# A fused layer's opening: transposed inputs, V's products chunk by chunk over all tokens, and the first norm's factor applied behind them

## The chip, the core and the metric

The kernel runs on one core of one Trainium2 chip. The metric is the device time of one execution in microseconds (us). A core has five engines that run side by side and wait for each other through semaphores: PE (TensorE, matrix products), ACT (ScalarE), DVE (VectorE), POOL (GpSimd) and SP (SyncE, which here only issues DMAs). Each engine takes its instructions strictly in their order, so an instruction that waits holds up everything behind it on its engine. Products land in eight PSUM banks, from which ACT and DVE read them.

## The reference

One layer over 512 tokens of width 1024, in float32. What matters for this change is its opening and one product near the middle:

```python
u = rms_norm(h, g_mix[i])          # x * rsqrt(mean(x*x) + eps) * g
z = u @ w_in[i]                    # q, k, v of two attentions, forget logits, gates
q_a, k_a, v_a, q_b, k_b, v_b, f_b, gate_logits = jnp.split(z, SPLIT_POINTS, axis=-1)
y_a = sliding_window_attention(...) @ w_br_swa[i]
y_b = forgetting_attention(..., f_b + b_forget[i]) @ w_br_fox[i]
...
h = h + ple_gate * (p[i] @ w_ple_proj[i])
```

The norm's factor, one number per token, multiplies every element of that token's row of `u`, and so it can also be multiplied onto a row of a product `(x * g) @ W` after the product. The kernel computes products to float32 accuracy: each operand is split into a high part (rounded to PE's fast float32 format) and the low rest, and each product is the sum of three, high by high, high by low, low by high. A split costs one ACT instruction (the high part) and one DVE instruction (the low part, which waits for the high one).

## The kernel before

Tokens are worked on in four blocks of 128 (`tb`), the width of 1024 in eight chunks of 128 (`k`). The opening, in a scratch pool `s0`, is the part that the change rewrites. For each block `tb`:

- `square1` forms the sum of squares of a row, `rms_rstd` (L359, L362, on POOL) raises it to the power -1/2, one number per token, and `scale1` (L454, DVE) multiplies block, factor and gain.
- `to_uT_pe` (L378) transposes the block on PE in eight 128x128 pieces, and `to_uT_split` (L70 on ACT, L71 on DVE) splits the transposed block out of PSUM into `uh` and `ul`.
- `v_mm` (L474) makes the block's V products for both attentions together with the forget logits: 648 columns, as 320 and 328 in two PSUM banks, eight chunks of three products each, so 48 products per block and 192 in all.
- `v_out` splits the products into `V2` and writes the logits `fl`.

V's weights are split once (`split_v`, L460 and L461). Before the first real product PE runs 20 transposes of an identity matrix (L501) and nine that bring the gain `g_mix` into the shapes wanted.

Behind the opening, `fill` multiplies `uh` and `ul` with the chunks of `w_in` one 128-column unit after the other (L74 to L76, PSUM tag `mm`, two banks): first `ka`, the keys of the sliding attention, 24 products that go through all eight `k`; then `qa`, and so on, mixed with the attention's steps. `unit(key)` hands out a unit's split weights (L324 on ACT, L325 on DVE, four pieces for early units) and splits two units ahead.

The order on PE and POOL is the order of the program text. Within the opening the order on ACT, DVE and SP is also that of the text; behind it a scheduler places instructions on these three and may move some of them between those of the opening. Tiles of later stages take over the memory of `s0` and wait until all that read it there is done.

Near the middle, `p_transposed` transposes `p` on PE (eight pieces, tile `p_tr`) and splits it for the product with `w_ple_proj`.

Of the kernel before, what the change touches and what calls it, by code (L numbers as in the profile page):

```python
# [8 lines left out]
F32 = mybir.dt.float32  # L9
# [5 lines left out]
P = 128  # L15
S = 512
# [10 lines left out]
N_WARM = (14, 3, 3)  # L27

# [22 lines left out]
def layer_kernel(ctx: ExitStack, tc: tile.TileContext, x, p, g_mix, w_in, b_forget, swa_sinks,  # L51
# [5 lines left out]
    p = p[0, 0]  # L57
# [354 lines left out]
    g_bc = s0.tile([P, D], F32, name="g_mix_bc")  # L412
    g_row = s0.tile([KT, P], F32, name="g_row")
    g_col = s0.tile([P, KT], F32, name="g_col")
    wv_h = s0.tile([P, KT, 648], F32R, name="wv_h")
    wv_l = s0.tile([P, KT, 648], F32R, name="wv_l")
    xts, wvs, xn1 = [], [], {}

    def load_x(tb):
        xt = s0.tile([P, D], F32, tag="xt", bufs=3, name=f"x_{tb}")  # L420
        for half in range(2):
            sl = slice(half * 512, half * 512 + 512)
            queue = nc.scalar if tb == 0 and half == 1 else nc.sync
            queue.dma_start(xt[:, sl], x[tb * P:(tb + 1) * P, sl])
            if tb == 0 and half == 0:
                nc.sync.dma_start(g_row, g_mix[0].rearrange("(k q) -> k q", q=P))
        xts.append(xt)

    def load_wv(k):
        src = w_in[k * P:(k + 2) * P, :].rearrange("(k q) c -> q k c", q=P)  # L430
        wv = s0.tile([P, 2, 648], F32, tag="wv_r", bufs=4, name=f"wv_{k}")
        nc.sync.dma_start(wv[:, :, 0:520], src[:, :, C_VB:C_VB + 520])
        nc.sync.dma_start(wv[:, :, 520:648], src[:, :, C_VA:C_VA + 128])
        wvs.append(wv)

    def square1(tb):
        acc = sm.tile([P, 2], F32, tag="acc1", name=f"acc1_{tb}")
        xn = xn1[tb] = s0.tile([P, D], F32, tag="xn", bufs=2, name=f"n1_{tb}_xn")
        nc.scalar.activation(xn[:, 0:512], xts[tb][:, 0:512], AF.Square, scale=1.0 / 32,
                             accum_out=acc[:, 0:1])  # L440
        if tb < 2:
            nc.vector.tensor_tensor_reduce(out=xn[:, 512:], in0=xts[tb][:, 512:],
                                           in1=xts[tb][:, 512:], scale=1.0 / D, scalar=0.0,
                                           op0=ALU.mult, op1=ALU.add, accum_out=acc[:, 1:2])
        else:
            nc.scalar.activation(xn[:, 512:], xts[tb][:, 512:], AF.Square, scale=1.0 / 32,
                                 accum_out=acc[:, 1:2])
        return acc

    def scale1(tb, acc):  # L450
        rs = rms_rstd(acc, f"n1_{tb}")
        for half in range(2):
            sl = slice(half * 512, half * 512 + 512)
            nc.vector.scalar_tensor_tensor(xn1[tb][:, sl], xts[tb][:, sl], rs,  # L454
                                           gps[half] if tb < 2 else g_bc[:, sl],
                                           ALU.mult, ALU.mult)

    def split_v(k):
        src = wvs[k // 2][:, k % 2]
        nc.scalar.copy(wv_h[:, k], src)  # L460
        nc.vector.tensor_tensor(wv_l[:, k], src, wv_h[:, k].bitcast(F32), ALU.subtract)  # L461
# [3 lines left out]
    def v_mm(tb, k, nk=1):  # L465

        ts_ = slice(tb * P, (tb + 1) * P)
        if k == 0:
            vps[tb] = (psA.tile([P, 320], F32, tag="mm", bufs=2, name=f"va_{tb}"),
                       psA.tile([P, 328], F32, tag="sc", bufs=3, name=f"vb_{tb}"))  # L470
        for n, (u, w) in enumerate(((uh, wv_h), (uh, wv_l), (ul, wv_h))):
            for kk_ in range(k, k + nk):
                for ps, c0, c1 in ((vps[tb][0], 0, 320), (vps[tb][1], 320, 648)):
                    nc.tensor.matmul(ps, u[:, kk_, ts_], w[:, kk_, c0:c1],  # L474
                                     start=kk_ == 0 and n == 0, stop=kk_ == KT - 1 and n == 2)

    def v_out(tb):
        pa, pb = vps[tb]
        for src, h0, n in ((pa, 0, 5), (pb[:, 0:192], 5, 3), (pb[:, 200:328], 8, 2)):
            v3 = src.rearrange("q (h d) -> q h d", d=HD)  # L480
            hi_lo(V2[tb][:, h0:h0 + n, 0:HD], V2[tb][:, h0:h0 + n, HD:2 * HD], v3)
        nc.vector.tensor_tensor(fl[:, tb, :], pb[:, 192:200], bf_bc, ALU.add)

    with tc.manual_schedule(engines={ET.Activation, ET.DVE, ET.SP}):
        load_x(0)
        load_wv(0)
        load_wv(2)
        load_x(1)
        load_wv(4)
        load_wv(6)  # L490
        load_x(2)
        load_x(3)
        bcast_row(bf_bc, b_forget[0])
        bcast_row(sink_bc, swa_sinks[0])


        warm = psA.tile([P, 4, P], F32, tag="tr", bufs=3, name="warm")

        def warm_up(n):
            for j in range(n):  # L500
                nc.tensor.transpose(warm[:, j % 4, :], ident, ident)  # L501
# [39 lines left out]
        for tb in range(1, NT):  # L541
# [8 lines left out]
            if tb == 2:  # L550
                unit("ka")
# [966 lines left out]
```

## Time and profile before

| | us |
|---|---|
| median of 3 runs | 715.99 (715.10 to 716.78) |
| the profiled execution | 717.25 |
| its span on the core | 715.3 |
| PE busy | 704.4 (98% of the span) |
| DVE, ACT, POOL busy | 532.7, 450.2, 84.8 |
| first V product on PE starts | 8.98 |
| first `ka` product on PE starts | 41.90 |
| first `qa` product on PE starts | 47.37 |

Times within the profile count from the span's start. A row of the timeline gives the start, the duration, the engine, the line of the program, the operation, what it writes and reads with sizes, and, where the engine stood idle before it, how long and what ended that. Where a row groups several instructions (x4), its duration reaches from the first's start to the last's end; neighbours on ACT and DVE overlap by some hundredths of a us. The chain of waits follows the end of the program back, at each step to what released the waiting instruction.

### The profile page before, as it was taken

The page shows a single profiled execution, that of the slowest core. Times are in us where ns is not written, and L with a number is a line of the kernel's source. Part 1 is how long each engine was busy: PE and PEld are TensorE (multiplying, and loading weights), DVE is VectorE, ACT ScalarE, POOL GpSimd, SP SyncE. Part 2 cuts the span into 40 slices and gives each one's busy share as a digit, 9 for nine tenths or more (in the row PEclk, how much of TensorE's full clock was granted, in tenths as well). Part 3 has the DMA queues.
Part 4 walks back from the last instruction along what each step waited for, and adds up shares of the span by engine and source line. Part 5 has one row for each costly group of instructions (what it writes and reads, how often), then busy time and mean ns, then how long its engine had stood idle before and what let it go on. Part 6 is the DMA issues. An engine that isn't in the chain of part 4 may idle for free.

```text
span 715.3 us, 11466 instructions
## 1 busy us (share of the span) xinstructions
PE 704.4 (98%) x4229; PEld 626.4 (88%) x4229; DVE 532.7 (74%) x908; ACT 450.2 (63%) x839; POOL 84.8 (12%) x124
## 2 busy tenths in 40 slices
PE   8999999999999999999999999999999999999995
PEld 7988888888888998888899889988999789988885
DVE  6557888877696556545789985899579966997565
ACT  6547888779863554344788736874477546875452
POOL 1011211100001200001510102010300021010101
PEclk9999999999999999999999999999999999999998
DMA  9256456670364795450885598739894699079002
GB/s 288 70 164 159 115 125 158 151 196 1 119 206 118 147 320 181 152 172 31 238 188 193 111 288 160 239 86 256 185 253 119 152 243 233 34 148 351 3 22 96
DMA packets 74055, 115.67 MB, mean 162 GB/s; under 512 B 6664, under 2 KB 44560, under 8 KB 74000
## 3 DMA queue, kind: packets, MB, share of 16 engines
q1 hardware_dynamic: 65936, 86.24, 38.0%
q0 software_dynamic: 7776, 28.32, 21.5%
q8 instruction: 33, 0.54, 0.3%
q10 hardware_dynamic: 288, 0.39, 0.2%
q14 instruction: 22, 0.18, 0.1%
HBM read 72.93 MB, written 4.19 MB: 108 GB/s over the span
## 4 chain that ended last, share of the span: by engine, by line
PE 86%; DVE 6%; DMA 4%; issue 2%; ACT 1%; POOL 0%; SPq 0%; POOLq 0%; DVEq 0%; ACTq 0%
PE pf L74 5%; PE pf L76 5%; PE pf L75 5%; PE s_6x L1331 3%; PE s_0x L1331 3%; PE h_sc L760 3%; PE s_2x L1331 2%; PE h_pv L830 2%; PE h_tr L818 2%; PE psm L76 2%; PE psm L74 2%; PE psy L74 2%; PE psy L75 2%; PE psm L75 2%; PE psy L76 2%
## 5 line engine op out<-in xcount | busy, mean ns | idle before, releaser
L298 POOL DMA_DIRECT2D wq<-wq x24 | 21.8, 936 | 166.8 <-DVE u70l L325 25.9
L778 ACT ACTIVATE s<-s,h_nm 128x128 f32<-128x128 f32 (+1 forms) x64 | 32.6, 512 | 5.9 <-DVE h_nm L771 5.1
L71 DVE TENSOR_TENSOR h_ptl<-h_tr,h_pth 128x512 fp32r<-128x512 f32 (+2 forms) x40 | 22.9, 604 | 4.0 <-ACT h_pth L70 3.6
L359 POOL TENSOR_SCALAR n_ms<-acc 128x1 f32<-128x1 f32 x15 | 5.6, 373 | 163.8 <-ACT junk L1083 105.4
L70 ACT CAST h_pth<-h_tr 128x512 fp32r<-128x512 f32 (+2 forms) x40 | 19.4, 523 | 1.8 <-PE h_tr L818 1.4
L70 ACT CAST u<-n_tr 128x512 fp32r<-128x512 f32 (+2 forms) x26 | 12.6, 519 | 11.8 <-PE n_tr L1139 5.6
L474 PE MATMUL va<-wv_h,u 128*128 128x320 f32 x64 | 20.0, 317 | 0.0
L818 PE MATMUL h_tr<-ident,s 128*128 128x128 f32 x136 | 19.6, 277 | 0.2
L474 PE MATMUL vb<-wv_h,u 128*128 128x328 f32 x64 | 19.6, 313 | 0.0
L71 DVE TENSOR_TENSOR u<-n_tr,u 128x512 fp32r<-128x512 f32 (+2 forms) x26 | 15.0, 603 | 5.8 <-ACT u L70 5.7
L298 POOL DMA_DIRECT2D wgw<-wgw x8 | 7.1, 971 | 102.3 <-DVE u25l L325 77.7
L1083 ACT ACTIVATE junk<-h_sb 128x512 f32<-128x512 f32 x16 | 10.1, 630 | 12.6 <-DVE h_sb L1073 10.1
L830 PE MATMUL h_pv<-h_pth,v 128*128 128x256 f32 (+1 forms) x64 | 17.3, 291 | 0.0
L830 PE MATMUL h_pv<-h_ptl,v 128*128 128x256 f32 (+1 forms) x64 | 16.9, 305 | 0.3 <-DVE h_ptl L71 0.3
L818 PEld LDWEIGHTS h_tr<-ident,s 128*128 128x128 f32 x136 | 15.1, 141 | 2.0 <-ACT s L798 0.5
L1420 DVE TENSOR_TENSOR sgp<-sgp,pp 128x512 f32<-128x512 f32 (+1 forms) x9 | 5.7, 632 | 14.2 <-ACT sgp L1419 14.2
L1073 DVE TENSOR_TENSOR h_sb<-psm,h_sb 128x512 f32<-128x512 f32 x8 | 5.5, 689 | 13.8 <-PE psm L76 13.8
L798 ACT ACTIVATE s<-s,h_rec 128x128 f32<-128x128 f32 (+2 forms) x32 | 14.2, 483 | 2.4 <-DVE h_rec L792 2.4
L840 DVE TENSOR_TENSOR h_ao<-h_pv,h_ao 64x512 f32<-64x512 f32 x16 | 10.9, 681 | 6.0 <-ACT h_ao L839 5.8
L766 DVE CUSTOM_DVE_ANT_0 s<-h_sc,causal 128x128 f32<-128x128 f32 (+3 forms) x32 | 13.8, 483 | 0.3 <-PE h_sc L760 0.3
L792 DVE RECIPROCAL h_rec<-h_den 128x4 f32<-128x4 f32 x16 | 3.0, 185 | 14.5 <-ACT s L778 14.3
L830 PEld LDWEIGHTS h_pv<-h_ptl,v 128*128 128x128 f32 x64 | 12.1, 188 | 1.7 <-DVE h_ptl L71 0.8
(1609 smaller groups left out, 2774.9 us busy)
## 6 DMA issues: line engine op xcount, KB each, us to landing
wq<-in_w_ff_dram SPq DMA_DIRECT2D x45, 512.0 KB, 5.9
wq<-wq POOLq DMA_DIRECT2D x24, 512.0 KB, 5.9
wq_c<-in_w_ff_dram SPq DMA_DIRECT2D x9, 512.0 KB, 6.7
wg<-in_w_in_dram SPq DMA_DIRECT2D x4, 1024.0 KB, 5.3
wgw<-in_w_in_dram SPq DMA_DIRECT2D x8, 512.0 KB, 4.7
wgw<-wgw POOLq DMA_DIRECT2D x8, 512.0 KB, 5.8
wmix<-in_w_mix_out_dram SPq DMA_DIRECT2D x4, 1024.0 KB, 5.1
wpg<-in_w_ple_gate_dram SPq DMA_DIRECT2D x4, 1024.0 KB, 8.6
```

Of the source, the lines that this page charges most:

```text
L70: nc.scalar.copy(hi, src)
L71: nc.vector.tensor_tensor(lo, src, hi.bitcast(F32), ALU.subtract)
L74: nc.tensor.matmul(ps, lh, rh, start=start, stop=False)
L75: nc.tensor.matmul(ps, lh, rl, start=False, stop=False)
L76: nc.tensor.matmul(ps, ll, rh, start=False, stop=stop)
L298: nc.gpsimd.dma_start(q, other, accum_op=ALU.add)
L474: nc.tensor.matmul(ps, u[:, kk_, ts_], w[:, kk_, c0:c1], start=kk_ == 0 and n == 0, stop=kk_ == KT - 1 and n == 2)
L760: nc.tensor.matmul(ps[:, off:off + n], qs[i][z][:, qb * P:(qb + 1) * P], kk[i][z][:, k0:k0 + n], start=z == 0, stop=z == 1)
L778: nc.scalar.activation(sl, sl, AF.Exp, bias=nm[:, qb:qb + 1], accum_out=den[:, qb:qb + 1])
L818: nc.tensor.transpose(tr[:, n, :], c["s"][:, o, :], ident)
L830: nc.tensor.matmul(pv[:, q0:q0 + nq, :], V2[kb][:, c["v"], :], t[:, o:o + nq, :], start=n == 0, stop=n == 2 * NT - 1, skip_group_check=True)
L1331: nc.tensor.matmul(bank[g // 2, "2" + bk, i], o, w, start=tg != "" and n == 0, stop=n == 5, skip_group_check=True)
```

## The change

Four inputs are added, laid out by the host without arithmetic: `x` transposed (`x_tr`), `p` transposed (`p_tr`), `g_mix` as a 128x8 array, and V's columns of `w_in` copied side by side (`w_v`), with the eight forget columns between the 448th and the 449th of the FoX part.

In the opening, PE transposes nothing but 20 identity pieces. `split_x` multiplies a chunk of `x_tr` by its gain and splits it (`xh`, `xl`). `v_mm` now runs chunk by chunk: for each `k` and each of the three products it goes over all four blocks, so V's sums take seven of the eight PSUM banks at once (the eighth serves the identity pieces and then the sum of squares). The products are without the norm's factor. The squares are formed per chunk (`square1`, ACT), added up on DVE, summed across partitions by two products with a matrix of ones behind the fourth chunk (`sum_squares`), and raised to the power -1/2 on POOL for all 512 tokens in every partition (a 128x512 array, `rsb`). `columns` picks the factor per token for `v_out`, which multiplies it on. `scale1` forms `uh` and `ul` for the later units: per chunk one DVE multiplication (L465), one ACT cast (L68), one DVE subtraction (L69). `p_split` replaces `p_transposed`: the two splits stay, the eight transposes go.

```diff
-N_WARM = (14, 3, 3)
+N_WARM = 20
...
+    def split_x(k):
+        g = g_col[:, k:k + 1]
+        nc.scalar.mul(xh[:, k], x_t[:, k], g)
+        nc.vector.scalar_tensor_tensor(xl[:, k], x_t[:, k], g, xh[:, k].bitcast(F32), ALU.mult,
+                                       ALU.subtract)
+    def split_w(k):
+        wvs[k] = [s0.tile([P, 648], F32R, tag=f"wv_{e}", bufs=3, name=f"wv_{e}{k}") for e in "hl"]
+        hi_lo(*wvs[k], wraw[k])
+    def square1(k):
+        if k == 0:
+            nc.scalar.activation(ssq, x_t[:, k], AF.Square)
+            return
+        t = s0.tile([P, S], F32, tag="t", bufs=2, name=f"sq_{k}")
+        nc.scalar.activation(t, x_t[:, k], AF.Square)
+        nc.vector.tensor_tensor(ssq, ssq, t, ALU.add)
+    def sum_squares():
+        ps = psA.tile([P, S], F32, tag="tr", bufs=3, name="ssq_ps")
+        for e in range(2):
+            nc.tensor.matmul(ps, ones_r, ssq_hl[:, e], start=e == 0, stop=e == 1)
+        nc.vector.tensor_scalar(ssq, ps, 1.0 / D, EPS, ALU.mult, ALU.add)
+        nc.gpsimd.tensor_tensor(rsb, ssq, mhalf.to_broadcast([P, S]), ALU.pow)
...
+    def scale1(k):
+        t = s0.tile([P, S], F32, tag="t", bufs=2, name=f"u1_{k}")
+        nc.vector.scalar_tensor_tensor(t, x_t[:, k], g_col[:, k:k + 1], rsb, ALU.mult, ALU.mult)
+        hi_lo(uh[:, k], ul[:, k], t)
...
+    def v_mm(tb, k, n):
+        u, w = ((xh, 0), (xl, 0), (xh, 1))[n]
+        for i, (ps, o, c0, c1) in enumerate(vps[tb]):
+            nc.tensor.matmul(ps[:, o:o + c1 - c0], u[:, k, tb * P:(tb + 1) * P],
+                             wvs[k][w][:, c0:c1], start=k == 0 and n == 0 and o == 0,
+                             stop=k == KT - 1 and n == 2, skip_group_check=True)
...
+        for k in range(4):
+            if k == 3:
+                square1(6)
+                square1(7)
+                hi_lo(ssq_hl[:, 0], ssq_hl[:, 1], ssq)
+            for n in range(3):
+                for tb in range(NT):
+                    v_mm(tb, k, n)
+            if k == 0:
+                split_w(3)
+                load_w(6)
+        sum_squares()
+        split_x(4)
+        split_w(4)
...
+        split_x(5)
+        split_w(5)
+        split_x(6)
+        scale1(0)
+        split_w(6)
...
+        split_x(7)
+        split_w(7)
+        for tb in range(NT):
+            columns(tb)
+        scale1(1)
+        scale1(2)
+        scale1(3)
+        unit("ka")
+        for tb in range(NT):
+            for k in (6, 7):
+                for n in range(3):
+                    v_mm(tb, k, n)
+            if tb == 0:
+                scale1(4)
+                v_out(0)
+                scale1(5)
+            if tb == 1:
+                scale1(6)
+                scale1(7)
+        for tb in range(1, NT):
+            v_out(tb)
...
-    def p_transposed():
+    def p_split():
         pth, ptl = pT[:] = [spare(4 + i, f"pT_{'hl'[i]}", (P, 2, S)) for i in range(2)]
         for k in range(2):
-            tr = psA.tile([P, 4, P], F32, tag="tr", bufs=3, name=f"p_tr{k}")
-            for tb in range(NT):
-                nc.tensor.transpose(tr[:, tb, :], p_sb[:, tb, k * P:(k + 1) * P], ident)
-            hi_lo(pth[:, k, :].rearrange("q (t c) -> q t c", c=P),
-                  ptl[:, k, :].rearrange("q (t c) -> q t c", c=P), tr)
+            hi_lo(pth[:, k], ptl[:, k], p_sb[:, k])
```

Where instructions stand is shown at three places. The first is DVE in the changed kernel around the sum of squares. `ssq_ps` is the PSUM bank with the sum, `xg_l` is `xl`, `u_0` the scaled chunk 0, `u_80` the tile of `uh` and `ul`, `rs_bc` is `rsb`; what a row waits for is named in its brackets.

```order
L69 TENSOR_TENSOR ssq_hl<-ssq,ssq_hl 128x512 [waits Activation_49]
L454 TENSOR_SCALAR ssq<-ssq_ps 128x512 [waits PE_49]
L433 SCALAR_TENSOR_TENSOR xg_l<-x_t,g_col,xg_h 128x512 [waits DMAHW0_49,Activation_49]
L69 TENSOR_TENSOR wv_l_312<-wv_167,wv_h_311 128x648 [waits DMAHW5_49,Activation_49]
L433 SCALAR_TENSOR_TENSOR xg_l<-x_t,g_col,xg_h 128x512 [waits DMAHW1_49,Activation_49]
L69 TENSOR_TENSOR wv_l_326<-wv_181,wv_h_325 128x648 [waits DMAHW7_49,Activation_49]
L433 SCALAR_TENSOR_TENSOR xg_l<-x_t,g_col,xg_h 128x512 [waits DMAHW3_49,Activation_49]
L465 SCALAR_TENSOR_TENSOR u_0_331<-x_t,g_col,rs_bc 128x512 [waits Pool_49]
L69 TENSOR_TENSOR u_80<-u_0_331,u_80 128x512 [waits Activation_49]
L69 TENSOR_TENSOR wv_l_336<-wv_222,wv_h_335 128x648 [waits DMAHW0_49,Activation_49]
```

The instruction that reads the sum waits for PE's two products behind the fourth chunk, and all splits of the chunks 4 to 7 stand behind it; the first use of POOL's power stands ahead of the last three splits.

The second place is the end of the opening on DVE in the changed kernel, from the third chunk's scaling to the first reading of V's sums (`v_0` is `V2[0]`, `v_141` the first PSUM bank of V; `u0l` to `u2l` are split weights of `ka` and `qa`).

```order
L465 SCALAR_TENSOR_TENSOR u_3_409<-x_t,g_col,rs_bc 128x512
L69 TENSOR_TENSOR u_80<-u_3_409,u_80 128x512 [waits Activation_49]
L323 TENSOR_TENSOR u0l<-wka,u0h 128x256 [waits DMAHW4_49,Activation_49]
L323 TENSOR_TENSOR u0l<-wka,u0h 128x256 [waits Activation_49] x3
L323 TENSOR_TENSOR u1l<-wqa_321,u1h 128x256 [waits DMAHW5_49,Activation_49]
L323 TENSOR_TENSOR u1l<-wqa_321,u1h 128x256 [waits Activation_49] x3
L323 TENSOR_TENSOR u2l<-wqa_321,u2h 128x256 [waits Activation_49] x4
L465 SCALAR_TENSOR_TENSOR u_4_459<-x_t,g_col,rs_bc 128x512
L69 TENSOR_TENSOR u_80<-u_4_459,u_80 128x512 [waits Activation_49]
L498 SCALAR_TENSOR_TENSOR v_0_87<-v_141,rs_104,v_0_87 128x5x64 [waits Activation_49]
L498 SCALAR_TENSOR_TENSOR v_0_87<-v_142,rs_104,v_0_87 128x2x64 [waits Activation_49]
```

Before, DVE read a block's sums while PE made the next block's products; now all four blocks are read at the end, behind the scalings and the first three units' splits, and the scalings of chunks 5 to 7 stand between the first block's reading and the others'.

The third place is PE in the changed kernel where V ends and `ka` (`pf_593`) begins.

```order
L485 MATMUL v_147<-wv_l_390,xg_h 128x456
L485 MATMUL v_145<-wv_l_390,xg_h 128x192
L72 MATMUL pf_593<-u_80,u0h 128x512 [waits DVE_49]
L73 MATMUL pf_593<-u_80,u0h 128x512
L74 MATMUL pf_593<-u_80,u0l 128x512
L72 MATMUL pf_593<-u_80,u0h 128x512
L73 MATMUL pf_593<-u_80,u0h 128x512
```

The first `ka` product waits for DVE, as it did before; its bank is the one that held `v_141`, the third of the tag `mm`'s turns, so the DVE instruction that frees it is the first `v_0` row of the second place.

More of the change, by code (lines that the diff above doesn't have):

```diff
@@ L450, in scale1 @@
[L450 to L461, printed above, removed]
@@ L463, in layer_kernel @@
-    vps = {}
[L465 to L475, printed above, removed]
@@ L493, in layer_kernel @@
+        sum_squares()
+        split_x(4)
+        split_w(4)
+        load_w(7)
         bcast_row(bf_bc, b_forget[0])
         bcast_row(sink_bc, swa_sinks[0])
[L497 to L501, printed above, removed]
-        warm_up(N_WARM[0])
-        ps = psA.tile([P, KT], F32, tag="mm", bufs=2, name="g_colps")
-        nc.tensor.transpose(ps, g_row, ident[0:KT, 0:KT])
@@ L538, in layer_kernel @@
-        to_uT(xn1[1], uh, ul, 1, psA, "n1_1")
-        v_mm(0, 6)
-        v_mm(0, 7)
-        for tb in range(1, NT):
-            if tb < NT - 1:
-                acc = square1(tb + 1)
-                scale1(tb + 1, acc)
-            v_out(tb - 1)
-            for k in range(KT):
-                v_mm(tb, k)
-                if k == 4 and tb < NT - 1:
-                    to_uT(xn1[tb + 1], uh, ul, tb + 1, psA, f"n1_{tb + 1}")
-            if tb == 2:
-                unit("ka")
-        v_out(NT - 1)
+        emit_dma(look["dma"])
```

164 lines of the change are left out of this document (84 added, 80 removed).

## The prediction

> **What bounds the kernel now.** First the page: its busy line and the chain of waits.
>
> ```profile
> span 715.3 us, 11466 instructions
> PE 704.4 (98%) x4229; PEld 626.4 (88%) x4229; DVE 532.7 (74%) x908; ACT 450.2 (63%) x839; POOL 84.8 (12%) x124
> PE 86%; DVE 6%; DMA 4%; issue 2%; ACT 1%; POOL 0%; SPq 0%; POOLq 0%; DVEq 0%; ACTq 0%
> ```
>
> PE carries 86% of the chain and is busy 98% of the span, so time that PE saves or loses in one stage normally comes through to the end. The change touches the opening, so I then asked the windows for that stage: up to the first V product, up to the first `ka` product, up to `ka`'s end (us from:to, its length, then busy time of PE, PEld, DVE, ACT, POOL, granted clock, DMA share, GB/s).
>
> ```profile
> 0.00:8.98 8.98, 7.54 (x37) 6.66 (x37) 2.96 (x8) 3.37 (x6) 1.56 (x8) 1.00 0.75 245
> 8.98:41.90 32.92, 32.30 (x217) 31.26 (x217) 23.46 (x52) 19.90 (x51) 3.04 (x6) 1.00 0.59 186
> 41.90:47.50 5.60, 5.60 (x27) 4.63 (x26) 3.45 (x17) 2.76 (x7) 3.37 (x7) 1.00 0.10 31
> ```
>
> V and the transposes occupy PE for 32.92 us, DVE for 23.46 of them. DVE has 26.4 us of work up to 41.90: it is not the bound, but it has only some 15 us to spare, and it runs in order. The timeline, and for the last row the chain in order of time (start, us, what), give the edges.
>
> ```profile
> 1.42 3.25 PE L501 MATMUL warm<-ident 128*128 128x128 f32 x14 [1.42 <-POOL ident masks.py:199]
> 1.24 1.28 ACT L439 ACT_TABLE_LOAD   x1 [1.24 <-PEq L1503]
> 4.10 0.63 ACT L439 ACTIVATE n_xn<-x 128x512 f32<-128x512 f32 x1 [1.58 <-DMA x<-in_x_dram]
> 36.83 0.31 PE L474 MATMUL va<-wv_l,u 128*128 128x320 f32 x1
> 41.75 0.31 PE L474 MATMUL vb<-wv_h,u 128*128 128x328 f32 x1
> 23.20 1.03 PE L378 MATMUL n_tr<-ident,n_xn 128*128 128x128 f32 x8
> 47.15 0.39 PE L76 MATMUL pf<-u,u0l 128*128 128x512 f32 x1
> 57.05 1.04 PE h_sc L760 x8
> ```
>
> From 36.83 to 41.75 there are 33 products, 0.149 us each. `ka`'s last starts at 47.15: 23 steps from 41.90, 0.228 each. The first identity pieces take 0.232 each, later transposes 0.11 to 0.13 (eight in 1.03).
>
> **What the change does on PE.** 20 identity pieces at 0.232 from 1.42 end at 6.1. The first product needs ACT's high parts of `x_0` and `w_0`: a transfer of x of this size landed at 4.10, a table load of 1.28 (ACT's, here behind the gain's DMA) and two ACT instructions of 0.7 (as L460 below) follow, so 6.1 to 7.0; I take 6.5, against 8.98. Four chunks of 24 products at 0.149 are 14.3, and the first few run at half rate (+0.7): 21.5. Two products with ones: 22.2 with the drain. Four more chunks and 0.4 of waiting for `xl_4` (DVE can split it only behind the sum of squares): V ends on PE at **36.9** against 42.1. That half of the change saves 5 us, by the three groups of transposes between 8.98 and 41.90, the earlier start and fewer stalls.
>
> **What it does on DVE.** The rows for each kind of instruction (groups: busy us, mean ns; then the timeline):
>
> ```profile
> L454 DVE SCALAR_TENSOR_TENSOR n_xn<-x,n_rs,g_mix_bc 128x512 f32<-128x512 f32 x4 | 2.8, 750 | 2.7 <-POOL n_rs L362 2.7
> L316 DVE SCALAR_TENSOR_TENSOR u165l<-wpg,g_ple_t,u165h 128x512 fp32r<-128x512 f32 x2 | 1.5, 751 | 2.5 <-ACT u165h L315 2.5
> L461 DVE TENSOR_TENSOR wv_l<-wv,wv_h 128x648 fp32r<-128x648 f32 x8 | 6.4, 830 | 0.3 <-ACT wv_h L460 0.3
> L460 ACT CAST wv_h<-wv 128x648 fp32r<-128x648 f32 x8 | 5.6, 732 | 3.5 <-DMA wv<-in_w_in_dram 3.5
> L71 DVE TENSOR_TENSOR attn<-h_ao,attn 128x512 fp32r<-128x512 f32 x8 | 5.5, 682 | 0.0
> L442 DVE CUSTOM_DVE_ANT_0 n_xn<-x 128x512 f32<-128x512 f32 x2 | 1.4, 682 | 0.0
> L70 ACT CAST attn<-h_ao 128x512 fp32r<-128x512 f32 x8 | 5.0, 620 | 0.9 <-DVE h_ao L840 0.9
> 33.67 1.42 DVE L325 TENSOR_TENSOR u0l<-wka,u0h 128x256 fp32r<-128x256 f32 x4
> 28.55 0.48 DVE L71 TENSOR_TENSOR v<-va,v 128x320 fp32r<-128x320 f32 x1
> 22.64 0.29 DVE L71 TENSOR_TENSOR v<-vb,v 128x128 fp32r<-128x128 f32 x1 [0.33 <-ACT v L70]
> ```
>
> Added: eight `xl` at 0.75, seven sums of squares, one low part and one scaling at 0.68, four `columns` at 0.36 (a 128x128 reduction, estimated from the 128x512 one of L442): 13.5. Removed: two reductions with their read-outs, 1.5. So 38.4 us of DVE work stands ahead of what 26.4 did, while PE's V now ends at 36.9. More decides the order. DVE has done the early splits by about 17, then stands before the sum of squares until PE's two products behind chunk 3, at **22.2**; everything else queues there. Back to back, an instruction starts 0.08 before its predecessor ends (four 128x256 in 1.42: 0.34 apart), so `xl` cost 0.67 and `wv_l` 0.75. From 22.2:
>
> - the scaling 0.6, four `xl` 2.7, four `wv_l` 3.0;
> - `scale1` for chunks 0 to 4. Its DVE multiplication, ACT cast and DVE subtraction depend on each other, and nothing stands between the two DVE instructions, so DVE idles through the cast (the row at 22.64 shows the same shape: DVE idle 0.33 behind a 0.27 cast). One chunk takes 0.75 + 0.62 + 0.60 + two handovers of 0.04 = 2.06; five take 10.3;
> - four `columns` 1.1 (pipelined), twelve pieces of `ka` and `qa` weights at 0.34: 4.1;
> - the first `v_out` piece 0.5.
>
> Sum 22.3: V's first PSUM bank comes free at **44.5**, and PE, done at 36.9, stands 7.7 us, since `ka`'s first product takes that bank. Before, it started at 41.90, so `ka` starts 2.6 later. Then `ka`'s fifth to eighth chunks wait for `uh` and `ul` of chunks 4 to 7: behind 44.1 (chunk 4) come `v_out(0)`'s rest, four pieces of weights, three more `scale1`: 8.0 us, so 52.2, and `ka`'s last three products end at 52.9 instead of 47.5 to 47.9: **5.0** later. `v_out` of the other blocks (some 4 us on DVE with weights between) follows at 52.2; `ka`'s result, in memory taken over from the opening, can be written only when that is done, about 57.4, and the first score product, 57.05 before, moves by 6.4. Two short waits later: 6.7. From there PE's order is the same in both, and in the walk the 6.7 stays.
>
> I walked both orders instruction by instruction with these durations. For the kernel before, the walk puts the first `ka` product at 42.2 and the first score product at 57.5 (trace 41.90, 57.05), so its differences hold to about half a us.
>
> **POOL's power of 128x512** stands in no row. The nearest (a median and its ends, then groups and single rows):
>
> ```profile
> L1173 POOL TENSOR_TENSOR u_s<-u_a,u_a x2: 1354/1492/1630, 340.4 to 348.2; 128x512 f32<-128x512 f32 x2
> L1183 POOL TENSOR_TENSOR u_s<-u_a,u_s x2: 1307/1624/1942, 349.6 to 356.2; 128x512 f32<-128x512 f32 x2
> 19.24 0.30 POOL L359 TENSOR_SCALAR n_ms<-acc 128x1 f32<-128x1 f32 x1 [5.29 <-ACT n_xn L446]
> 19.63 0.56 POOL L362 TENSOR_TENSOR n_rs<-n_ms,mhalf 128x1 f32<-128x1 f32 x1
> ```
>
> From below: an addition of that shape, 1.3 to 1.9. From above: a power of one column costs 0.26 more than an addition of one; were that paid for each of 512 columns, 135 us. It starts at 22.9 and is first wanted at 26.3 (DVE has `xl` and `wv_l` to do), so 3.4 us are hidden, and beyond that each us delays DVE's chain by one. I take the rows of the same shape, so nothing. **`p`**: eight transposes go.
>
> ```profile
> L1206 PE MATMUL p_tr<-ident,p_sb x8: 273/273/273, 309.6 to 310.3; 128*128 128x128 f32 x8
> ```
>
> At 0.11 apart they are 0.9 us on a busy PE. The two splits stay. DMA, by the window in which the opening's loads run:
>
> ```profile
> 10.00:20.00 10.00, 9.38 (x61) 8.49 (x61) 8.74 (x14) 8.50 (x19) 1.98 (x4) 1.00 1.09 327
> ```
>
> At 327 GB/s a chunk's 0.26 and 0.33 MB take 1.8 us, PE 3.6 per chunk: hidden; without that cover PE would wait for the loads 1:1.
>
> **Sum:** +6.7 - 0.9 = +5.8 us on the profiled execution's 717.25, so 723.0; the median lies 1.3 under that execution: **722**.
>
> One rule speaks further against it. The row at 1.42 shows slow pieces while the granted clock is 1.00. The Trainium skill, TensorE: Matmul & The Clock Gate, The HAM clock gate, says that PE's clock halves after about 3.4 us of idleness and needs as long to recover. By it the first 3.4 us behind the 7.7 us stall would run at half rate; since `ka` there waits for chunks 4 to 7 until 52.2 anyway, the sum would become 722 to 723.
>
> **Rivals.** (a) *POOL's power decides.* Point 3.4 us; price each us beyond: 10 us give 729, 17 give 736. For it: the 0.56 against 0.30, and the 26.3 at which DVE stands still until it comes; against it: 1.3 to 1.9 for a shape that is the same. (b) *Faster: PE's stream decides.* If DVE keeps up, only PE's own 5.2 (42.1 to 36.9) and 0.9 count: 710. It needs V's first bank free by 36.9, 7.7 us sooner than the chain of DVE has it; for it: DVE is idle 26% of the span, and 9 us of it in the window of V (32.92 less 23.46); against: every term of that chain is a row, and the scheduler has put it in this order. (c) *A draw:* the chain is 5 or 6 us shorter than summed, the earlier end of V pays for the rest: 715 to 717.
>
> **How the numbers follow.** My forecast (719 to 725) 0.52, (a) 0.28, (b) 0.13, (c) 0.07. The forecast's own range comes from the first product's 6.1 to 7.0, half a us of the walk and a us of the cold clock. The range for 8 in 10 goes from 716 to 736: it leaves out (b), half of (c), and powers over 17 us, about 0.07. What a measurement can tell from no change is 0.2%, 1.4 us: faster 0.13, same 0.07, slower 0.80.
>
> **What would show it.** V's last product near 37; PE idle before the first `ka` product for 7 to 8 us, ended by DVE's first `v_out` piece near 44.5; DVE idle some 5 us before the scaling (L454) and 0.8 before each subtraction of `scale1`; `ka` ending near 53; the power under 3.4 us on POOL. It is wrong if the first `ka` product starts before 41, or if PE stands before chunk 6 of V (then the power is long).

## The result, and the profile after

| | before | after |
|---|---|---|
| median, us | 716.13 (715.10 to 716.78) | 812.26 (811.90 to 813.93) |
| ratio, 95% interval | | 1.1348 (1.1328 to 1.1369) |
| profiled execution, us | 717.25 | 811.90 |
| its span, us | 715.3 | 810.2 |
| mean granted clock | 0.997 | 0.942 |

The change makes the kernel 96 us slower; 722 was predicted, with 716 to 736 as the range. The page of the changed kernel answers the first fence of the prediction (span, busy time by engine, some of the rows of 40 equal slices in tenths, the chain of waits by engine):

```profile
span 810.2 us, 11393 instructions
PE 710.4 (88%) x4182; PEld 629.1 (78%) x4182; DVE 543.9 (67%) x927; ACT 456.1 (56%) x841; POOL 163.7 (20%) x118
...
PE   9400048899999999999999999999999999999996
...
POOL 0899911120100000200013101210020003011101
PEclk9855568999999999999999999999999999999998
...
PE 62%; POOL 11%; DVE 9%; issue 8%; DMA 6%; ACT 4%; SPq 0%; POOLq 0%; ACTq 0%; DVEq 0%
```

PE's busy time has hardly changed (704.4 before, 710.4 now); it lies in a span 95 us longer, with three slices of 20 us in which PE does nothing. In those slices POOL is full, and POOL has come from 0% to 11% of the chain. The groups say with what (line, engine, operation, tiles, size, count | busy, mean ns | idle time before them and what ended it):

```profile
L455 POOL TENSOR_TENSOR rs_bc<-ssq,mhalf 128x512 f32<-128x512 f32 x1 | 82.4, 82390 | 21.0 <-DVE ssq L454 21.0
L465 DVE SCALAR_TENSOR_TENSOR u<-x_t,g_col,rs_bc 128x512 f32<-128x512 f32 x8 | 6.0, 745 | 78.2 <-POOL rs_bc L455 78.2
L485 PE MATMUL v<-wv_h,xg_h 128*128 128x320 f32 (+1 forms) x64 | 13.0, 332 | 77.6 <-ACT wv_h L68 77.6
```

One instruction, the power of 128x512, takes 82.39 us. DVE's first multiplication by the factor (`scale1`, L465) waits 78.2 us for it. PE is named as waiting for ACT's `wv_h`, and ACT did nothing long: that cast only stands behind ACT's cast of the scaled chunk 0, which waits for DVE, which waits for POOL. The windows show the standstill and what follows it (from:to, length, busy time of PE, PEld, DVE, ACT, POOL with counts, granted clock, DMA share, GB/s):

```profile
30.00:104.00 74.00, 0.00 (x0) 0.00 (x0) 0.00 (x0) 0.00 (x0) 74.00 (x1) 0.52 0.04 15
104.00:110.00 6.00, 2.96 (x11) 2.96 (x12) 4.37 (x12) 2.50 (x4) 0.92 (x1) 0.50 0.00 1
120.00:125.00 5.00, 2.20 (x5) 1.81 (x6) 3.71 (x10) 2.93 (x8) 0.00 (x0) 0.50 1.07 354
```

For 74 us no engine but POOL works, and the transfers have all but stopped (15 GB/s). By then PE has made 144 of V's 192 products, those of chunks 0 to 5, so it stands before chunk 6: the prediction's own sign that the power is long. PE resumes at a granted clock of 0.50.

By marks on PE's timeline the loss builds up in steps: the first `ka` product comes 80.9 us later than before (122.80 against 41.90), the first score product 88.6 later, the first `psy` product 90.4, the start of the feed-forward stage (`s_0x`) 90.6, the last stage's first product (`psgt`) 94.3. So not all of it is the power. The experiments take the steps apart.

### The profile page after: what moved, and what is told of

It reads as the page before. It is cut to its first block, busy times and chain, and to the rows that moved or that the text cites. A ratio compares the mean times of both kernels' runs of the same rounds, so it can differ in the third digit from the quotient of the medians.

```text
span 810.2 us, 11393 instructions
## 1 busy us (share of the span) xinstructions
PE 710.4 (88%) x4182; PEld 629.1 (78%) x4182; DVE 543.9 (67%) x927; ACT 456.1 (56%) x841; POOL 163.7 (20%) x118
## 4 chain that ended last, share of the span: by engine, by line
PE 62%; POOL 11%; DVE 9%; issue 8%; DMA 6%; ACT 4%; SPq 0%; POOLq 0%; ACTq 0%; DVEq 0%
POOL rs_bc L455 10%; PE pf L73 4%; PE pf L72 4%; PE pf L74 4%; PE s_0x L1359 3%; PE s_2x L1359 2%; DMA wq<-wq 2%; DMA wq_t<-wq 2%; PE h_sc L792 2%; PE psy L72 2%; PE psm L74 2%; PE psy L74 2%; PE psm L72 2%; PE psm L73 2%; PE psy L73 2%
## 5 line engine op out<-in xcount | busy, mean ns | idle before, releaser
L455 POOL TENSOR_TENSOR rs_bc<-ssq,mhalf 128x512 f32<-128x512 f32 x1 | 82.4, 82390 | 21.0 <-DVE ssq L454 21.0
L485 PE MATMUL v<-wv_h,xg_h 128*128 128x320 f32 (+1 forms) x64 | 13.0, 332 | 77.6 <-ACT wv_h L68 77.6
L485 PEld LDWEIGHTS v<-wv_h,xg_h 128*128 128x128 f32 x64 | 10.7, 203 | 78.5 <-ACT wv_h L68 78.3
L68 ACT CAST u<-u 128x512 fp32r<-128x512 f32 x16 | 9.8, 619 | 102.0 <-DVE u L465 96.1
L465 DVE SCALAR_TENSOR_TENSOR u<-x_t,g_col,rs_bc 128x512 f32<-128x512 f32 x8 | 6.0, 745 | 78.2 <-POOL rs_bc L455 78.2
L357 POOL TENSOR_SCALAR n_ms<-acc 128x1 f32<-128x1 f32 x11 | 3.9, 358 | 144.8 <-ACT junk L1115 107.0
L69 DVE TENSOR_TENSOR h_ptl<-h_tr,h_pth 128x512 fp32r<-128x512 f32 (+2 forms) x40 | 22.9, 604 | 3.5 <-ACT h_pth L68 3.3
L68 ACT CAST h_pth<-h_tr 128x512 fp32r<-128x512 f32 (+2 forms) x40 | 19.4, 523 | 1.9 <-PE h_tr L850 1.5
L1115 ACT ACTIVATE junk<-h_sb 128x512 f32<-128x512 f32 x16 | 10.1, 629 | 15.4 <-DVE h_sb L1105 12.9
L798 DVE CUSTOM_DVE_ANT_0 s<-h_sc,bswa 128x256 f32<-128x256 f32 (+1 forms) x32 | 10.8, 382 | 6.4 <-PE h_sc L792 6.4
L69 DVE TENSOR_TENSOR u<-u,u 128x512 fp32r<-128x512 f32 x16 | 10.8, 686 | 4.8 <-ACT u L68 4.8
```

Source lines behind the costliest of these rows:

```text
L68: nc.scalar.copy(hi, src)
L69: nc.vector.tensor_tensor(lo, src, hi.bitcast(F32), ALU.subtract)
L455: nc.gpsimd.tensor_tensor(rsb, ssq, mhalf.to_broadcast([P, S]), ALU.pow)
L798: nc.vector.tensor_tensor_reduce(out=s[:, o:o + n], in0=ps[:, off:off + n], in1=c["bias"](qb), scale=1.0, scalar=NEG, op0=ALU.add, op1=ALU ...
```

## Experiments

The times of one table row belong together with runs of the kernel before on the same chip.

| kernel | median, us | before, us | ratio, 95% interval |
|---|---|---|---|
| the change | 812.26 | 716.13 | 1.1348 (1.1328 to 1.1369) |
| e1_pieces | 815.16, one run | 715.74 | |
| e2_add | 735.00 | 715.74 | 1.0274 (1.0259 to 1.0289) |
| e3_add_pad | 733.14 | 715.74 | 1.0239 (1.0224 to 1.0254) |
| e4_before_shift | 721.15 | 715.74 | 1.0075 (1.0058 to 1.0092) |
| e5_narrow | 724.98 | 716.09 | 1.0114 (1.0099 to 1.0130) |
| e6_order | 717.49 | 716.09 | 1.0020 (1.0010 to 1.0030) |
| e7_p | 714.75 | 716.09 | 0.9980 (0.9971 to 0.9988) |
| e8_warm | 732.01 | 716.09 | 1.0230 (1.0206 to 1.0253) |
| e9_inputs | 718.89 | 715.82 | 1.0045 (1.0030 to 1.0060) |
| e10_last | 715.16 | 715.82 | 0.9993 (0.9982 to 1.0003) |
| e11_rs1 | 727.01 | 716.20 | 1.0147 (1.0132 to 1.0162) |
| e12_rs1_last | 725.01 | 716.20 | 1.0119 (1.0102 to 1.0136) |

The theory from the traces of the two kernels: the power is slow by the column, everything else of the prediction holds, and the drift in the feed-forward stage has to do with memory addresses. All on-chip tiles that follow the pool of small tiles lie 64 bytes lower in the change, because a tile of that pool is no longer needed. The rival: the power's time is something else (paid once), and the products by chunks lose time of their own that the power hides.

### e1_pieces: what the power's time goes by

```diff
-        nc.gpsimd.tensor_tensor(rsb, ssq, mhalf.to_broadcast([P, S]), ALU.pow)
+        for a, b in ((0, 32), (32, 128), (128, 256), (256, 512)):
+            nc.gpsimd.tensor_tensor(rsb[:, a:b], ssq[:, a:b], mhalf.to_broadcast([P, b - a]),
+                                    ALU.pow)
```

> The same power, cut into four instructions of 32, 96, 128 and 256 columns. If its time goes by the column (82.39 us for 512, 0.161 us each): about 5.5, 15.8, 21 and 41.5 us, in all 82 to 84 us and the kernel within 1 us of the change's 812. If most of it is paid once for an instruction, whatever its size (the one-column power's 0.56 us speaks against it): four times 82 us, and the kernel near 1060 us. If it is paid once at the first use of the function: the first piece near 80 us, the others under 1.5 us each.

The groups of this kernel on POOL, shapes kept apart:

```profile
L456 POOL TENSOR_TENSOR rs_bc<-ssq,mhalf 128x256 f32<-128x256 f32 x1 | 41.1, 41125 | 0.0
...
L456 POOL TENSOR_TENSOR rs_bc<-ssq,mhalf 128x128 f32<-128x128 f32 x1 | 20.7, 20725 | 0.0
L456 POOL TENSOR_TENSOR rs_bc<-ssq,mhalf 128x96 f32<-128x96 f32 x1 | 15.7, 15653 | 0.0
...
L456 POOL TENSOR_TENSOR rs_bc<-ssq,mhalf 128x32 f32<-128x32 f32 x1 | 5.9, 5884 | 21.0 <-DVE ssq L454 21.0
```

From 128 to 256 columns the time grows by 20.40 us, 0.159 per column; from 32 to 96 by 9.77, 0.153. The four together take 83.4 us, the whole took 82.4. The price is paid for each column, and the rivals (once per instruction, once at the first use) are out. The kernel, run once, takes 815.2 us, 3 more than the change where at most 1 was expected; 0.8 of that lies ahead of `ka`, the rest is not explained.

### e2_add: the power taken away, its place kept

```diff
-        nc.gpsimd.tensor_tensor(rsb, ssq, mhalf.to_broadcast([P, S]), ALU.pow)
+        nc.gpsimd.tensor_tensor(rsb, ssq, mhalf.to_broadcast([P, S]), ALU.add)
```

> The change with the power's function replaced by an addition of the same shape, operands and place; the norm's factor is then left out of the result. If the power's length is the whole of the miss: the prediction's own sum, 722 us, with the first product of ka near 44 us, PE idle 7 to 8 us before it and a clock that falls once at most. If the last stage's weights moved by 64 bytes cost what the trace of the change shows there (its feed-forward stage starts 90.6 us late and ends 94.9 late, so 4.3 us): 726 us. If the products by chunks lose time of their own that the long power hid: above 730 us.

The addition takes 1.47 us, as the prediction's rows for that shape said:

```profile
22.73 1.47 POOL L455 TENSOR_TENSOR rs_bc<-ssq,mhalf 128x512 f32<-128x512 f32 x1 [21.21 <-DVE ssq L454]
```

The kernel takes 735.0 us. So the power is worth 77 us of the 96, and 19 are left where the prediction had 6. Of the three readings on record only the third, above 730, has the number; where the time is lost, the next runs show. PE's clock fell twice, where one fall at most was expected.

### e3_add_pad and e4_before_shift: 64 bytes

```diff
+    sm.tile([P, 2], F32, tag="acc1", name="line_d")
```

in the kernel of e2_add, and in the kernel before the reverse:

```diff
-        acc = sm.tile([P, 2], F32, tag="acc1", name=f"acc1_{tb}")
+        acc = s0.tile([P, 2], F32, tag="acc1", bufs=2, name=f"acc1_{tb}")
```

> The kernel of e2_add with an unused tile of 64 bytes per partition in the pool of small tiles, which puts all later tiles back to the addresses that they have in the kernel before. If the addresses are what made the feed-forward stage longer: 4 us less than e2_add, 722 us if that gave 726, and the 256-wide products of that stage back at one per 0.113 us. If the stage was longer for another cause (order of transfers, clock): the same time as e2_add within 1 us.

> The kernel before with one small tile (the norm's sums, two buffers of 32 bytes) taken from the pool of small tiles to that of the first stage: all later tiles then lie 64 bytes lower, as in the change, and nothing else is altered. If the addresses make the feed-forward stage longer: about 4 us slower than the kernel before, 720 us, the whole of it after the attention. If they do not: 716 us.

The kernel before with all later tiles 64 bytes lower (one small tile has moved into the opening's memory, nothing else is altered) is 5.4 us slower than the kernel before; about 4 were expected. The chain of waits of the kernel before in its second feed-forward quarter (start, us, what, with the count of products):

```profile
434.23 2.72 PE ('f1', 2)y L918 x24
436.95 2.72 PE ('f1', 2)z L918 x24
...
445.11 2.72 PE ('f1', 2)x L918 x24
447.83 2.72 PE ('f1', 3)x L918 x24
450.55 2.87 PE ('f1', 2)x L918 x24
...
459.07 2.83 PE ('f1', 3)z L918 x24
```

and the same groups in e4_before_shift:

```profile
436.43 2.88 PE ('f1', 2)y L918 x24
439.31 2.74 PE ('f1', 2)z L918 x24
...
447.63 2.88 PE ('f1', 2)x L918 x24
450.51 2.88 PE ('f1', 3)x L918 x24
453.39 2.74 PE ('f1', 2)x L918 x24
...
461.57 2.72 PE ('f1', 3)z L918 x24
```

Each group is 24 products, 256 columns wide. Of the quarter's twelve, six are slower in e4_before_shift (2.86 to 2.88 us instead of 2.72 to 2.77; 0.120 us for a product instead of 0.113), and the last four are faster (2.72 to 2.74 instead of 2.83 to 2.87), so this quarter alone loses only 0.4 us (33.6 against 33.2). Over all 56 groups of this kind, each taken from its first product's start to its last's, it is 150.8 us against 147.3. The other traces agree: the four kernels with the lower addresses (the change, e1_pieces, e2_add, e4_before_shift) lie between 150.8 and 151.9, the ten others between 146.7 and 147.9. The granted clock is 1.00 throughout this quarter in the kernel before and in e4_before_shift. Why the address matters, no run shows. In the kernel with the addition the same 64 bytes were worth less, 2.5 us by the ratios (1.0274 against 1.0239; 3.4 between the two profiled spans), where 4 were expected. So the addresses are a real cost, and not the whole drift: e3_add_pad is still at 733.

Its trace shows how far the prediction's sum holds. The timeline of e3_add_pad, in the order of the prediction's steps (start, us, engine, line, what, and the idle time before it):

```profile
21.91 0.69 DVE L455 TENSOR_SCALAR ssq<-ssq_ps 128x512 f32<-128x512 f32 x1 [3.78 <-PE ssq_ps L454]
28.27 0.69 DVE L69 TENSOR_TENSOR u<-u,u 128x512 fp32r<-128x512 f32 x1 [0.69 <-ACT u L68]
36.80 0.48 PE L486 MATMUL v<-wv_l,xg_h 128*128 128x456 f32 x2
44.10 0.80 DVE L499 SCALAR_TENSOR_TENSOR v<-v,rs,v 128x320 fp32r<-128x320 f32 x2
44.70 0.80 PE L72 MATMUL pf<-u,u0h 128*128 128x512 f32 x1 [7.42 <-DVE v L499]
52.85 0.39 PE L74 MATMUL pf<-u,u0l 128*128 128x512 f32 x1
57.77 0.60 ACT L672 ACTIVATE ka_h<-pf 128x512 fp32r<-128x512 f32 x1 [1.00 <-DVE fl L502]
58.40 1.17 SPq L666 DMA_DIRECT2D kah<-ka_h  x2
66.97 0.30 PE L793 MATMUL h_sc<-kah,qa 128*128 128x128 f32 x1 [3.41 <-issue]
```

DVE waits 3.78 us for the sum of squares, and 0.69 inside each `scale1`; V ends on PE at 37.3, PE stands 7.42 us for DVE's first `v_out` piece, and `ka` ends at 53.2. DVE's wait for the sum is shorter than the 5 us predicted; the rest is within 0.4 us of the prediction's numbers. Then it parts: the first score product comes at 66.97, 10.1 us later than the 56.91 before, where 6.4 was predicted. It follows ACT's `ka_h`, which waits until DVE has written the last `fl`, and SP's moves behind it. The same three places in the kernel before:

```profile
47.71 0.59 ACT L639 ACTIVATE ka_h<-pf 128x512 fp32r<-128x512 f32 x1
48.33 1.17 SPq L633 DMA_DIRECT2D kah<-ka_h  x2
56.91 0.30 PE L760 MATMUL h_sc<-kah,qa 128*128 128x128 f32 x1
```

From SP's first move to the first score product it is 8.58 us before and 8.57 now: SP issues eight moves of `ka` and four of `qa` in one row, at about 0.6 us each. So the score product is late by exactly as much as the first move.

### e11_rs1: four columns in another place

The factor's four columns (`rs1`) lie in memory that `ka_h` takes over, and every `v_out` reads them. In e11_rs1 they lie in the padding tile:

```diff
-    rs1 = s0.tile([P, NT], F32, name="rs1")
+    rs1, _ = (sm.tile([P, NT], F32, tag="acc1", name=n) for n in ("rs1", "line_d"))
```

> The kernel of e3_add_pad (an addition in the power's place, addresses as before) with one thing more: the four columns of the norm's factor lie in the padding tile instead of in the opening's memory, so the tile for ka's high part no longer takes over memory that the last v_out still reads. If ka's evacuation waits for that memory and SP's moves, ten in one row behind it, set the first score product: ka's high part near 54 us instead of 57.8, the first score product near 63.4 instead of 67.0, no second fall of the clock, and the kernel 4 to 5 us faster than e3_add_pad, 728 to 729. If the moves wait for something else: 733.

```profile
53.33 0.59 ACT L671 ACTIVATE ka_h<-pf 128x512 fp32r<-128x512 f32 x1
...
53.95 1.18 SPq L665 DMA_DIRECT2D kah<-ka_h  x2
...
62.77 0.30 PE L792 MATMUL h_sc<-kah,qa 128*128 128x128 f32 x1
```

`ka_h` is written as soon as `ka` ends, the first score product is 5.9 us later than before instead of 10.1, and the kernel takes 727.0 us, 6.6 less than e3_add_pad by the ratios: more than the 4 to 5 expected. Part of the gain is PE's clock. In e3_add_pad the wait of 3.41 us before the first score product was followed by a second fall of the clock. The windows of e3_add_pad, and behind them the one of the kernel before for the same work:

```profile
44.70:48.00 3.30, 3.30 (x9) 2.64 (x10) 3.07 (x9) 2.23 (x6) 0.00 (x0) 0.56 0.73 237
...
68.50:72.00 3.50, 3.50 (x15) 3.01 (x14) 1.21 (x8) 2.52 (x10) 0.85 (x1) 0.57 0.00 0
```

```profile
58.50:62.00 3.50, 3.50 (x21) 3.04 (x20) 2.50 (x15) 2.60 (x11) 1.28 (x2) 1.00 0.73 252
```

At 0.57 PE works on 15 products in 3.5 us, at 1.00 on 21. By PE's marks this took 1.6 us more (the `psy` stage starts 11.7 us late in e3_add_pad, the score products 10.1); in e11_rs1 both are 5.9 late.

### e8_warm: the clock by itself

```diff
+        for j in range(N_IDLE[0]):
+            nc.tensor.transpose(idle[:, j % 4 * P:(j % 4 + 1) * P], ident, ident)
         for tb in range(1, NT):
             v_out(tb)
...
+        if i == 0:
+            for j in range(N_IDLE[1]):
+                nc.tensor.transpose(idle[:, j % 4 * P:(j % 4 + 1) * P], ident, ident)
```

> The kernel of e3_add_pad with dummy transposes into an unused bank in PE's two waits, 50 ahead of ka's first product and 22 ahead of the first score product. If the halved clock behind each of the two waits costs time: the first score group runs at full clock and the kernel is 1.5 to 2 us faster, 731; the first wait's half-clock products cost nothing, since ka's last chunks wait for DVE. If the clock is only a companion of the waits: 733.

732.0 us against 733.1, with intervals that overlap: unclear. In its profile the first score group ran at full clock, but a fall of 3.4 us came a little earlier, behind `ka`'s last products (granted clock 0.67 between 55 and 60 us). This execution was the slowest of the four, 736.2 us: its score products came 3.1 us later than those of e3_add_pad, and PE then waited 1.1 us for ACT. So it does not isolate the clock; what the clock costs by itself rests on the windows above.

### e5_narrow and e6_order: the change with a short power

Here the power runs on four columns with tokens on partitions, and PE spreads the factor; the norm's factor and result are the change's own, and the four column reductions and the split of the sum fall away:

```diff
-            nc.tensor.matmul(ps, ones_r, ssq_hl[:, e], start=e == 0, stop=e == 1)
-        nc.vector.tensor_scalar(ssq, ps, 1.0 / D, EPS, ALU.mult, ALU.add)
-        nc.gpsimd.tensor_tensor(rsb, ssq, mhalf.to_broadcast([P, S]), ALU.pow)
+            nc.tensor.matmul(ps[:, tb:tb + 1], ssq[:, tb * P:(tb + 1) * P],
+                             ones_r[:, 0:1].bitcast(F32), start=True, stop=True)
+        nc.vector.tensor_scalar(ms1, ps[:, 0:NT], 1.0 / D, EPS, ALU.mult, ALU.add)
+        nc.gpsimd.tensor_tensor(rs1, ms1, mhalf.to_broadcast([P, NT]), ALU.pow)
...
+            nc.tensor.transpose(rsb[:, tb * P:(tb + 1) * P],
+                                rs1[:, tb:tb + 1].to_broadcast([P, P]), ident)
```

> The change, right in its result, with the power on 128x4 instead of 128x512: four products with a column of ones give the sums with tokens on partitions, POOL raises four columns, and four transposes on PE spread them over a PSUM bank that the scaling reads; the four column reductions fall away; addresses as before. If the power goes by the column, 128x4 take about 1 us (0.40 + 4 x 0.161) and the kernel is at the time of the addition with the padding, 733 us, less about 1 us of DVE for the four reductions: 731 to 733. If POOL has another cost in this function (a first use, a table), more than 740.

725.0 us: 9 less than e3_add_pad by the ratios, where 1 or 2 were expected. The power of 128x4 takes 1.48 us. The surplus agrees with what e11_rs1 won: here too the four columns lie outside the opening's memory, and `ka_h` is written at 54.02.

e6_order changes the order of DVE and ACT in it. PE's two steps for the factor also come earlier, the sum ahead of chunk 3's products and the spreading ahead of chunk 4's, and the scaled chunks get a third buffer:

```diff
-        scale1(1)
-        scale1(2)
-        scale1(3)
-        unit("ka")
+        scale_a(1)
+        split_x(7)
+        scale_b(1)
+        scale_a(2)
...
+        v_out(0)
+        unit("ka")
+        scale_a(5)
+        scale_a(6)
+        scale_b(5)
+        scale_a(7)
+        scale_b(6)
+        scale_b(7)
```

(`scale_a` is the multiplication of `scale1`, `scale_b` its split.)

> The kernel of e5_narrow with DVE's and ACT's order changed and nothing removed: the sum of squares two thirds of a chunk earlier on PE, each scale1 started before the low part of the one ahead, v_out(0) and the splits of ka's weights ahead of the last three scale1. If DVE's chain sets ka's start, as the prediction has it: PE's 7.4 us of idle time before ka shrink to under 2, ka starts near 38 us and the first score product near 57 instead of 67; the kernel near 721, and level with the kernel before if the later waits shrink with it. If something else holds PE there (a transfer of weights, a bank), less than 2 us are won: above 729.

PE's timeline at the first `ka` product, and all of PE's waits between 5 and 75 us (us in total, times, longest):

```profile
36.95 0.41 PE L72 MATMUL pf<-u,u0h 128*128 128x512 f32 x1
```

```profile
PE h_sc L798 <- DMA qa<-qa_h: 1.1, 1, 1.1
PE v L487 <- ACT wv_h L68: 0.4, 1, 0.4
PE pf L73 <- DVE u L69: 0.2, 1, 0.2
```

The waiting ahead of `ka` (6.1 us in e5_narrow, 7.4 in e3_add_pad) is gone, and `ka` starts 4.9 us earlier than in the kernel before. So the order of DVE's chain held PE there; how much of it is due to the factor's coming earlier, this run does not separate. The first score product is 2.6 us earlier than in the kernel before (one near 57 was expected), and at the start of the feed-forward stage it is 3.5 us ahead. By its median it ends at 717.5, 1.4 behind, where 721 was expected: the feed-forward stage gives back all of what was won.

### e7_p: the last part of the change alone

```diff
-            tr = psA.tile([P, 4, P], F32, tag="tr", bufs=3, name=f"p_tr{k}")
-            for tb in range(NT):
-                nc.tensor.transpose(tr[:, tb, :], p_sb[:, tb, k * P:(k + 1) * P], ident)
...
+            hi_lo(pth[:, k], ptl[:, k], p_sb[:, k])
```

in the kernel before.

> The kernel before with the last part of the change alone: p given transposed, its eight transposes gone. The prediction's term: 0.9 us faster, 714.8. Rival: the transposes stand in PE's stream for nothing (DVE or a load ends last there): no difference. If the feed-forward stage's later half of the drift comes with the changed inputs: slower by 1 to 3 us.

714.75 us, 1.4 faster by the ratio (0.9 to 2.1). By PE's marks 0.9 of it is at the product with `p`, as predicted. It is the lowest time of this study.

### e9_inputs, e10_last, e12_rs1_last: where the inputs lie

e9_inputs is the kernel before with three more inputs that nothing reads:

```diff
-_INS = ["x", "p", "g_mix", "w_in", ...
+_INS = ["x", "x_tr", "w_v", "g_mix_c", "p", "g_mix", "w_in", ...
```

and e10_last is e6_order, e12_rs1_last is e11_rs1, with those inputs at the end of the list.

> The kernel before with three more inputs given and not read: the transposed x, V's gathered weights and the gain as columns, at the places in the list of inputs that the change gives them. If the feed-forward stage's drift (3 us in e6_order behind equal on-chip addresses) comes from where the inputs lie in the chip's memory: 2 to 4 us slower than the kernel before, 718 to 720, with transfers of weights landing later. If it comes from the program: the kernel before's time, 716.

> The kernel of e6_order with the three added inputs at the end of the list of inputs instead of ahead of the weights, nothing else. If the place of the inputs sets the drift: 3 to 4 us less than e6_order, 713 to 714, faster than the kernel before. If not: as e6_order, 717.5.

> The kernel of e11_rs1 with the three added inputs at the end of the list of inputs. If what e6_order and e10_last showed holds here too: 2 to 3 us less than e11_rs1. If the place of the inputs matters only by chance: the same time.

e9_inputs is 3.2 us slower than the kernel before (2.1 to 4.3), with the same instructions and on-chip addresses; its times scatter from 716.7 to 722.7, those of the kernel before from 714.9 to 717.5. Moving the inputs to the end wins 1.9 us in e10_last by the ratios and 2.0 in e12_rs1_last. In the first pair the intervals do not touch; in the second they overlap by a little. With it e10_last is level with the kernel before (0.9982 to 1.0003). The sizes expected were right for e9_inputs and e12_rs1_last, too large for e10_last. That the place of the inputs matters is shown; through what is not. The issues of DMAs in e6_order (in the kernel before both of these took 5.9 us to landing):

```profile
wq<-in_w_ff_dram SPq DMA_DIRECT2D x45, 512.0 KB, 6.6
wq<-wq POOLq DMA_DIRECT2D x24, 512.0 KB, 6.1
```

do not explain it. They look like later transfers of weights, but with the inputs at the end e10_last has 6.5 and 6.1 for the same rows, and e9_inputs has 5.9 for both in its one profile, an execution of 716.8.

One more thing differs between executions. Between 7.0 and 10.3 us PE works on 23 products in the profile of e11_rs1 and on 14 in that of e12_rs1_last, at a granted clock of 1.00 by the rows of both:

```profile
7.00:10.30 3.30, 3.30 (x23) 3.24 (x23) 3.03 (x6) 3.30 (x6) 0.00 (x0) 1.00 1.04 384
```

```profile
7.00:10.30 3.30, 3.30 (x14) 3.25 (x13) 3.03 (x6) 3.30 (x6) 0.00 (x0) 1.00 1.03 380
```

V ends on PE at 37.2 in the one and 39.2 in the other, and from `ka` on e12_rs1_last's marks are 2 us later. The profiles of e5_narrow, e8_warm and e10_last have 14 as well; those of the change and of e6_order have 24.

## Why the prediction was wrong

**The step that failed: POOL's power.** The prediction bounded it by 1.3 and 135 us and took the lower end, "the rows of the same shape, so nothing". It took 82.4, 78.1 of them in sight (`ka` starts at 44.73 in e2_add, at 122.80 with the power). The upper bound was the nearer one, and its row was in the fence: a power of one column took 0.26 us more than an addition of one, though both have the same shape. A row of the same shape and another function says what the shape costs, not what the function costs. Rival (a) had the mechanism, the place, the point (3.4 us; 4.2 measured) and the price of 1 us for each us beyond, but its examples and the range stopped at 17 us, and longer powers were given 0.07. With the 82.4 measured, (a)'s own rule gives 801 (722 + 82.4 - 3.4). The prediction's other sums hold, but for two slips: 44.5 less 36.9 is 7.6, and its range leaves out 0.235 by its own chances, not 0.2.

**PE's half of the change: right.** First product 6.4 (6.5 predicted), sum of squares on DVE at 21.9 (22.2), V's end on PE at 37.3 (36.9).

**DVE's chain to `ka`: right, term by term.** With the short addition, V's first bank came free at 44.7 (44.5), PE stood 7.42 us (7.7), `ka` ended at 53.2 (52.9). e6_order supports the cause: e5_narrow's work in another order, and the wait is gone.

**First score product "+6.4": the mechanism right, the size wrong.** The prediction had `ka`'s result written "about 57.4" because of the memory taken over (57.77 measured). It did not carry this on: SP's moves follow in one row, and the score product moves by as much as the first of them, 10.1. e11_rs1, which removes the wait for memory, has 5.9. The wait also cost a second fall of PE's clock, 1.6 us.

**"From there the 6.7 stays": wrong.** The feed-forward stage, with the same products, is longer in the changed kernel. 64 bytes of address (5.4 us in the kernel before, 2.5 in the kernel with the addition) and the added inputs ahead of the weights (3.2 and 2.0) both matter. The prediction looked at the order of instructions alone, and these are not in it.

**`p`: right.** -0.9 predicted, -0.9 by PE's marks, -1.4 in the time.

**The clock rule.** The Trainium skill, TensorE: Matmul & The Clock Gate, The HAM clock gate, was cited for a clock that halves after about 3.4 us of idleness. The rows agree for the long waits: 0.52 in the 74 us of standstill, 0.56 behind the wait of 7.42, 0.57 behind that of 3.41. They do not for e8_warm: its clock fell too (0.67 between 55 and 60 us), where no wait in the 8 us before was longer than 0.6 us. The prediction said that the half rate in `ka`'s first products costs nothing, since `ka` waits for DVE further on; `ka`'s end, 0.3 us from the time summed from DVE's rows, fits that. That a second wait and a second fall would follow, it missed.

By the ratios, then, of the 96.5 us: 76.9 the power, 2.5 the 64 bytes, 6.6 the memory of the four columns with what hangs on it, 2.0 the place of the inputs. 8.5 are left in e12_rs1_last. The DVE chain that was predicted, less the gain at `p`, explains 5.0 of these (e11_rs1 is that much behind when the feed-forward stage begins; the profile of e12_rs1_last, with its slow start, is 7.1 behind). Some 3.5 us within the feed-forward stage stay open. In e11_rs1 PE waits there three times, for 1.4 to 1.5 us, ahead of a 24-product group; it waits for an ACT copy that stands behind splits of weights, and some of these splits waited for their transfers. No run separates this further.

Had the power been as short as an addition, the change would still have been slower, 735: at the upper edge of the range, on the side that was given 0.80. That this lies inside the range is in part luck: of the 13 us between 722 and 735 a good part comes from the addresses, the place of the inputs and the second fall of the clock, which the prediction does not have.

## What to carry to other kernels

An operation of which the trace has only a small instance is priced by what its elements cost there, against another function on the same elements; if the two bounds are a factor of 70 apart, the function has to be measured before anything else is summed up, and the range has to hold the far end. A reduction with one number per token is best raised to a power while it is one number per token, 128x4 here and 1.48 us, and spread afterwards. When an opening is rewritten, follow what its last readers keep occupied: four columns of memory cost 6.6 us here, by way of a queue of moves.

## What the runs showed of the hardware that was not expected

- A power on POOL: 0.15 to 0.16 us for each further column of 128 partitions (5.9, 15.7, 20.7, 41.1 and 82.4 us for 32, 96, 128, 256 and 512 columns), where an addition of 512 columns takes 1.47. The first columns cost more: 0.56 us for one, 1.48 for four.
- On-chip tiles 64 bytes lower: the 56 groups of 24 products of 256 columns take 150.8 us instead of 147.3, at the same granted clock, and the kernel 5.4 us longer.
- Three inputs that nothing reads, placed ahead of the weights in the list of inputs: 3.2 us longer, and a wider scatter.
- The first products of V at two speeds in executions of this family of kernels: 23 or 24 of them between 7.0 and 10.3 us, or 14, with V's end at 37 or at 39 us.
